# The last up-projection pair of a ConvFFN as a seven-product block pair, joined to a reordered start of the down projection

## The chip, the cores and the metric

One core of one Trainium2 chip runs the whole kernel. The metric is the device time of one execution in microseconds; the figure of a kernel is the median over its runs. Engines are named as in the profile: PE (TensorE, matmuls), DVE (VectorE), ACT (ScalarE), POOL (GpSimd), SP (SyncE, which here only issues DMAs).

## The reference

The reference is one layer of a streaming encoder on 1024 tokens of width 1024: a mixer (attention and a state-space part), and then a gated feed-forward block. All is float32. The change lies in the feed-forward block:

```python
hid = xn @ w_up                                    # 1024 x 5632
hp = jnp.pad(hid, ((0, 0), (CONV_WIDTH - 1, 0), (0, 0)))
conv = conv_b + sum(hp[:, j:j + seq_len] * conv_w[j] for j in range(CONV_WIDTH))
val, gate = jnp.split(conv, 2, axis=-1)
return (jax.nn.silu(gate) * val) @ w_down          # 2816 x 1024
```

The result is added to the residual h, and a last RMSNorm follows.

## The kernel before, in words

Every float32 product is made of three matmuls on split operands: hi·hi, hi·lo and lo·hi. The hi part is a cast (ACT, `S.copy`), the lo part is the difference from it, a subtraction with two operands in SBUF (`split_lo`, L137), on VectorE or GpSimd.

**Up projection.** The 5632 columns of `w_up` are worked as 22 pairs c = 0 to 21; a pair is 128 gate columns and the 128 value columns that belong to them. Pairs 0, 1, 2 and 21 are plain: 144 matmuls 344 or 342 columns wide. Pairs 3 to 20 are block pairs (`block_pair`, `seven`): the 2 × 2 block product of gate and value weights by two halves of the depth and the tokens is made of seven products in place of eight, each on two pieces of 258 and 256 columns, 168 matmuls in all. A block pair needs four sums of weight blocks (GpSimd, `combine`), seven casts and splits, and additions of the results into hg and hv (VectorE, L242). Then the convolution is a scaling on ACT (L1501) and two steps on VectorE for gate and for value, silu on ACT (L1312), a multiplication (L1313; on GpSimd, for the last pair on VectorE), and a store of 128 rows to the DRAM buffer `a_d` (`glue`).

**Down projection.** The 22 row blocks of 128 are joined to eleven j. They are worked in four groups, (8, 9), (7, 0, 1), (2, 3, 4) and (5, 6, 10). A group is again seven products p, in the order 0, 4, 1, 2, 5, 3, 6 (4, 3 and 6 go on in PSUM banks of earlier products), each on four tiles t of 128 tokens, with three matmuls 512 wide for each j. `forms(p, j)` loads the two operands of a product (`ar` of the activations, `wr` of the weights; SP queue), casts them (ACT, L1583) and splits them: on GpSimd for p = 0, 4, 5, else on VectorE. `product` issues the matmuls (L1697 to L1699) and takes the results from PSUM: copies into u2 for the first product, else additions into u2 and hs on VectorE (L1707). The sums of activations for the later groups are on GpSimd too (L1570 to L1576).

A scheduler sorts the instructions of each engine by a simulated timeline. `after(a, b)` puts a behind b in that sorting alone; it is an order, and makes no semaphore between engines. On the chip each engine then works its list from the front.

Of the kernel before, what the change touches and what calls it, by code (L numbers as in the profile page):

```python
# [9 lines left out]
F = mybir.dt.float32  # L10
# [9 lines left out]
P = 128  # L20
# [38 lines left out]
def block_kernel(ctx, tc, x, meta, xbt, x0t, g1t, w_q, w_k, w_v, w_f, w_u, w_g, b_f, w_ao, lam_d, bw_d, cw_d,  # L59
# [142 lines left out]
    def to_feature(xs, n, dhi, dlo, col, bank=st_ps):  # L202
# [9 lines left out]
        return los  # L212

    def m_ps():
        return pp.tile([P, 512], F, tag="mm", name="mm", bufs=3)

    def seven(pl, A, B, kh, pieces, shift, top, bot):
# [26 lines left out]
        for q in st:  # L244
            S.copy(q["c1"], prod(q, "a", m_ps, A11, B11))
        for q in st:
# [1046 lines left out]
    def up_raw(m):  # L1293
        raw = rp.tile([P, KD, P], F, tag="raw", name="raw", bufs=3)
        SY.dma_start(raw, w_up[m])
        return raw
# [14 lines left out]
    def glue(g_, v_, c):  # L1311
        S.activation(g_, g_, AF.Silu)  # L1312
        (V if c == NFF - 1 else GP).tensor_tensor(v_, v_, g_, ALU.mult)  # L1313
        l_, r_ = HALF
        rows = a_d[P * c:P * c + P]
        if c % 2 == 0 and c // 2 in SUMMED:
            SY.dma_start(rows[:, l_], v_[:, l_])
            even[0] = v_
            return
        (S if c == NFF - 1 else SY).dma_start(rows, v_)  # L1320
        if c // 2 not in SUMMED:
            return
        e_, j = even[0], c // 2
        GP.tensor_tensor(e_[:, l_], e_[:, l_], e_[:, r_], ALU.subtract)
        GP.tensor_tensor(g_[:, l_], v_[:, r_], e_[:, l_], ALU.add)
        GP.tensor_tensor(e_[:, r_], v_[:, r_], e_[:, r_], ALU.subtract)
        GP.tensor_tensor(g_[:, r_], g_[:, l_], v_[:, l_], ALU.subtract)
        for p, t_ in ((1, e_[:, l_]), (2, g_[:, l_]), (3, e_[:, r_]), (6, g_[:, r_])):
            SY.dma_start(s_d[p][P * j:P * j + P], t_)

    even, SUMMED = [None], (7, 8, 9)

    def conv_out(m, tag):
        if m % NFF == NFF - 1:
# [106 lines left out]
    HS = LQ - NH  # L1441
    PIECES = [(0, 258), (258, 256)]
    st_t = ExitStack()
    tq = pool(st_t, "tforms", side="left")
    T = [[tq.tile([P, KH, NH], R, name=f"t{i}{w}") for w in "hl"] for i in range(4)]

# [43 lines left out]
    def block_pair(c):  # L1490
# [6 lines left out]
        seven(ha, A, [B11, T3, T2, T1, B21, T4, B22], KH, PIECES, HS, hg, hv)  # L1497
        res = []
        for h_, m, tag in ((hg, NFF + c, "og"), (hv, c, "ov")):
            o = conv_out(m, tag)  # L1500
            S.activation(o, h_[:, :SEQ], AF.Identity, bias=cwc(3, m), scale=cwc(0, m))  # L1501
            for j in (1, 2):
                V.scalar_tensor_tensor(out=o, in0=h_[:, j:SEQ + j], scalar=cwc(j, m), in1=o,  # L1503
                                       op0=ALU.mult, op1=ALU.add)
            res.append(o)
        glue(*res, c)

# [4 lines left out]
    for c in range(3, NFF - 1):  # L1512
        block_pair(c)
    st_t.close()
    plain_pair(NFF - 1)

    down1 = pool(ctx, "down1", side="left")
    small = [down1.tile([P, 4, 512], R, name=f"op{q}") for q in range(4)]  # L1520
    ops = [[t_[:, w] for w in range(4)] for t_ in small]
    ops += featq
    dpool = {}
    pairs = {}
# [5 lines left out]
    def raw_tile(j, k, h_):  # L1530
        if (k, h_) not in pairs.setdefault(j, {}):
            pairs[j][k, h_] = dpool[turn_of[j] % 4 // 2].tile([P, 512], F, tag=f"a{k}{h_}", name="ar", bufs=2)
        return pairs[j][k, h_]

    def behind(ld, j):
        if h_load and j in groups[1]:
            after(ld, h_load[-1])

    LAST = NFF // 2 - 1
    FROM = {0: (0, 0), 4: (1, 0), 5: (1, 1)}  # L1540

# [19 lines left out]
    def forms(p, j):  # L1561
        b_ = down1.tile([P, 512], F, tag="w", name="wr", bufs=8)
        behind(SY.dma_start(b_, w_block(*own_w[p], j) if p in own_w else t_d[p][P * j:P * j + P]), j)
# [30 lines left out]

    first_add, first_copy, cuts = [], [], []

# [81 lines left out]
    def product(g, p, slots, first, last):  # L1678
# [61 lines left out]
    def prepare():  # L1740

        while len(ready) < (len(items) if first_add else 3):
# [7 lines left out]
            ready[g, p] = [forms(p, j) for j in groups[g]]  # L1750

    dpool[0] = down1
# [6 lines left out]
    dn.tile([P, 512], F, tag="a00", name="hold", bufs=2)  # L1759
    sq = dn.tile([P, 512], BF, name="sq")  # L1760
    eps = dn.tile([P, 1], F, name="eps")
    V.memset(eps, EPS)
    u2 = [dn.tile([P, 512], F, name=f"u2{c}") for c in range(4)]
    hs = [dn.tile([P, D], F, name=f"hs{c}") for c in range(4)]
    hs += [dn.tile([P, D], F, name=f"hs{c}") for c in range(4, KD)]
    small2 = [dn.tile([P, 4, 512], R, name=f"op{q}") for q in range(4, 6)]
    ops += [[t_[:, w] for w in range(4)] for t_ in small2]
    for c in range(4):
        h_load.append(SY.dma_start(hs[c], h_d[P * c:P * c + P]))
    for g, p in turns:  # L1770
        prepare()
# [416 lines left out]
```

## Time and profile before

| | us |
|---|---|
| median of 3 runs (1425.15 to 1426.94) | 1426.13 |
| profiled execution, its own time | 1427.24 |
| its span, first to last instruction | 1425.5 |
| PE busy | 1410.6 (99%) |
| DVE busy | 1070.3 (75%) |
| POOL busy | 764.2 (54%) |
| ACT busy | 709.0 (50%) |

Busy times are sums over the whole span, and the mean granted clock of TensorE is 0.998 of full speed. An engine that is busy for less than the span costs time only where another waits for it; so the table says who is full, and the rows further down say where the others come near it.

### The profile page before, as it was taken

To read this page: it belongs to the slowest core of one execution; us is meant where nothing else is said; L and a number is where in the kernel's file an instruction comes from. 1 tells how busy PE (TensorE), PEld (TensorE's weight loads), DVE (VectorE), ACT (ScalarE), POOL (GpSimd) and SP (SyncE) were. 2 spreads that over 40 slices of the span, in tenths; PEclk is the share of its full clock that TensorE was granted. 3 is DMA by queue.
4 is the path that set the end of the run, shared out by engine and by line. 5 is a ranking of instruction groups with operands and counts; after the bars stand their busy time and mean duration, and the time that the engine had idled before them with its cause. 6 is when DMAs were issued, how large, how long until landed. Compare 5 with 4: busy or idle time off the path is not lost.

```text
span 1425.5 us, 26319 instructions
## 1 busy us (share of the span) xinstructions
PE 1410.6 (99%) x9607; PEld 1336.1 (94%) x9607; DVE 1070.3 (75%) x2048; ACT 709.0 (50%) x1381; POOL 764.2 (54%) x872
## 2 busy tenths in 40 slices
PE   8999999999999999999999999999999999999997
PEld 8999999988999999999889999999999999888886
DVE  7999889843667675655479977788886776788867
ACT  7647575423555555534546444344444345644444
POOL 1542257642466556326771334545555545888795
PEclk9999999999999999999999999999999999999999
DMA  8685644530156531087953246666753327864443
GB/s 298 176 203 147 160 106 133 172 119 31 53 156 161 127 111 57 23 287 267 216 161 124 73 114 183 183 173 177 178 142 113 98 79 258 327 205 133 129 94 118
DMA packets 93318, 216.17 MB, mean 152 GB/s; under 512 B 14802, under 2 KB 22610, under 8 KB 92804
## 3 DMA queue, kind: packets, MB, share of 16 engines
q1 hardware_dynamic: 74340, 170.28, 36.3%
q0 software_dynamic: 17696, 41.29, 15.1%
q10 hardware_dynamic: 1152, 2.91, 0.7%
q8 instruction: 76, 1.25, 0.4%
q14 instruction: 54, 0.44, 0.1%
HBM read 170.88 MB, written 71.71 MB: 170 GB/s over the span
## 4 chain that ended last, share of the span: by engine, by line
PE 95%; DMA 2%; issue 1%; ACT 1%; DVE 0%; POOL 0%; POOLq 0%; DVEq 0%; SPq 0%
PE mm L174 5%; PE mm L176 5%; PE mm L175 5%; PE sp L236 4%; PE sp L237 4%; PE sp L238 4%; PE tp L236 3%; PE tp L237 3%; PE tp L238 3%; PE mm L238 3%; PE mm L236 3%; PE mm L237 3%; PE po L966 3%; PE tp L920 2%; PE mm L1699 2%; PE mm L1698 2%
## 5 line engine op out<-in xcount | busy, mean ns | idle before, releaser
L174 PE MATMUL mm<-xhi,whi 128*128 128x342 f32 (+2 forms) x480 | 156.1, 325 | 0.0
L175 PE MATMUL mm<-xlo,whi 128*128 128x342 f32 (+2 forms) x480 | 155.4, 324 | 0.0
L176 PE MATMUL mm<-xhi,wlo 128*128 128x342 f32 (+2 forms) x480 | 154.6, 322 | 0.5 <-DMA wlo<-in_w_g_dram 0.5
L1313 POOL TENSOR_TENSOR ov<-ov,og 128x1024 f32<-128x1024 f32 x21 | 50.8, 2421 | 119.7 <-ACT og L1312 117.4
L137 DVE TENSOR_TENSOR sw<-sf,sw 128x512 fp32r<-128x512 f32 x72 | 73.4, 1020 | 46.2 <-ACT sw L1304 45.1
L1304 ACT CAST sw<-sf 128x512 fp32r<-128x512 f32 x72 | 44.9, 624 | 108.9 <-POOL sf L1451 80.1
L176 PEld LDWEIGHTS mm<-xhi,wlo 128*128 128x128 f32 x480 | 90.4, 188 | 1.3 <-DMA wlo<-in_w_g_dram 0.8
L174 PEld LDWEIGHTS mm<-xhi,whi 128*128 128x128 f32 x480 | 90.4, 188 | 1.1 <-issue 0.6
L175 PEld LDWEIGHTS mm<-xlo,whi 128*128 128x128 f32 x480 | 90.4, 188 | 0.4
L1451 POOL TENSOR_TENSOR sf<-raw,sf 128x512 f32<-128x512 f32 x36 | 62.9, 1748 | 38.8 <-DVE sw L137 38.7
L1451 POOL TENSOR_TENSOR sf<-raw 128x512 f32<-128x512 f32 x36 | 49.1, 1363 | 60.0 <-ACT ov L1361 21.5
L238 PE MATMUL mm<-xhi,sw 128*128 128x258 f32 (+1 forms) x288 | 81.0, 281 | 0.0
L236 PE MATMUL mm<-xhi,sw 128*128 128x258 f32 (+1 forms) x288 | 80.8, 280 | 0.0
L237 PE MATMUL mm<-xlo,sw 128*128 128x258 f32 (+1 forms) x288 | 80.7, 280 | 0.0
L883 ACT ACTIVATE pt<-pt,mx 128x400 f32<-128x400 f32 (+5 forms) x72 | 53.1, 737 | 45.2 <-DVE mx L876 44.9
L1503 DVE SCALAR_TENSOR_TENSOR ov<-hv,cwt,ov 128x1024 f32<-128x1024 f32 x36 | 69.9, 1942 | 0.4 <-ACT ov L1501 0.4
L885 POOL TENSOR_SCALAR pt<-pt,mx 128x400 f32<-128x400 f32 (+5 forms) x72 | 51.8, 721 | 33.3 <-DVE mx L884 28.3
L1304 ACT CAST sw<-raw 128x512 fp32r<-128x512 f32 x70 | 43.0, 621 | 45.0 <-PE sp L238 23.1
L137 DVE TENSOR_TENSOR sw<-raw,sw 128x512 fp32r<-128x512 f32 x70 | 57.9, 831 | 4.3 <-ACT sw L1304 4.0
L137 DVE TENSOR_TENSOR tl<-tp,th 128x512 fp32r<-128x512 f32 (+1 forms) x80 | 50.7, 634 | 12.2 <-ACT th L923 11.6
L923 ACT CAST th<-tp 128x512 fp32r<-128x512 f32 (+1 forms) x80 | 43.4, 543 | 32.1 <-PE tp L920 22.7
L852 POOL CAST qz<-q 64x128 fp32r<-64x128 f32 (+1 forms) x72 | 20.2, 283 | 67.2 <-PE sp L871 65.7
(722 smaller groups left out, 5727.2 us busy)
## 6 DMA issues: line engine op xcount, KB each, us to landing
raw<-in_w_up_dram SPq DMA_DIRECT2D x44, 512.0 KB, 3.7
t_d<-in_w_dn_dram POOLq DMA_DIRECT2D x44, 256.0 KB, 6.9
wr<-t_d SPq DMA_DIRECT2D x44, 256.0 KB, 3.4
ar<-a_d SPq DMA_DIRECT2D x41, 256.0 KB, 5.3
a_d<-ov SPq DMA_DIRECT2D x18, 512.0 KB, 2.6
wr<-in_w_dn_dram SPq DMA_DIRECT2D x33, 256.0 KB, 3.8
t_d<-in_w_dn_dram SPq DMA_DIRECT2D x22, 256.0 KB, 4.3
t_d<-t_d SPq DMA_DIRECT2D x22, 256.0 KB, 4.7
```

The costliest lines, as they stand in the source:

```text
L137: return eng.tensor_tensor(out_, src, hi.bitcast(F), ALU.subtract)
L174: yield PE.matmul(ps, whi[:, i, :], ahi[:, i], start=(i == 0), stop=False)
L175: yield PE.matmul(ps, whi[:, i, :], alo[:, i], start=False, stop=False)
L176: yield PE.matmul(ps, wlo[:, i, :], ahi[:, i], start=False, stop=(i == k - 1))
L236: PE.matmul(ps, a[0][:, i], bh, start=(i == 0 and not joins), stop=False, skip_group_check=True)
L237: PE.matmul(ps, a[0][:, i], bl, start=False, stop=False, skip_group_check=True)
L238: PE.matmul(ps, a[1][:, i], bh, start=False, stop=(i == kh - 1), skip_group_check=True)
L883: ends[:] = rd, S.activation(pt[:n, :kc], pt[:n, :kc], AF.Exp, bias=low, scale=-1.0, accum_out=nm[:n, 0:1])
L885: sc_.append(GP.tensor_scalar(pt[:n, :kc], pt[:n, :kc], nm[:n, 1:2], 1.0, ALU.mult, ALU.mult))
L1304: S.copy(hi, src)
L1451: sums.append(GP.tensor_tensor(f_, a, b, op))
L1503: V.scalar_tensor_tensor(out=o, in0=h_[:, j:SEQ + j], scalar=cwc(j, m), in1=o, op0=ALU.mult, op1=ALU.add)
```

## The change

Pair 21 becomes a block pair. The function of a block pair is cut in two: `block_pair` now ends with hg and hv, and `conv_pair` does the convolution and calls `glue`. For pair 21 the first product of the down projection stands between them in the code. The operands of that product for (8, 9) go into a quarter of the xhi and xlo buffers that is free during the pair, so they are loaded and split earlier. In the order asked for, the two scalings of pair 21 stand ahead of the first copies of product 0, silu behind them; GpSimd's splits for group 1 stand behind all of the splits of group 0 by either engine. The store of pair 21's rows goes from ACT's queue to GpSimd's. The two last additions of product 2 stand behind the splits of product 3.

```diff
@@ seven
-            S.copy(q["c1"], prod(q, "a", m_ps, A11, B11))
+            kept["c1"] = S.copy(q["c1"], prod(q, "a", m_ps, A11, B11))
@@ glue
-        S.activation(g_, g_, AF.Silu)
+        silu = S.activation(g_, g_, AF.Silu)
+        for cp_ in first_copy:
+            after(silu, cp_)
         (V if c == NFF - 1 else GP).tensor_tensor(v_, v_, g_, ALU.mult)
...
-        (S if c == NFF - 1 else SY).dma_start(rows, v_)
+        kept[c] = (GP if c == NFF - 1 else SY).dma_start(rows, v_)
@@ block_pair, cut in two
-        res = []
-        for h_, m, tag in ((hg, NFF + c, "og"), (hv, c, "ov")):
-            o = conv_out(m, tag)
-            S.activation(o, h_[:, :SEQ], AF.Identity, bias=cwc(3, m), scale=cwc(0, m))
+        return hg, hv
+
+    def conv_pair(c, hg, hv, behind=()):
+        res = {}
+        halves = ((hg, NFF + c, "og"), (hv, c, "ov"))
+        for h_, m, tag in halves[::-1] if behind else halves:
+            res[tag] = o = conv_out(m, tag)
+            act = S.activation(o, h_[:, :SEQ], AF.Identity, bias=cwc(3, m), scale=cwc(0, m))
+            if behind:
+                for cp_ in first_copy:
+                    after(cp_, act)
+                for hi in casts[:4]:
+                    after(act, hi)
             for j in (1, 2):
...
     for c in range(3, NFF - 1):
-        block_pair(c)
-    st_t.close()
-    plain_pair(NFF - 1)
...
+        conv_pair(c, *block_pair(c))
...
+    ops = quarter(0, 1)
@@ forms
+            if j in groups[0] and p == 0:
+                after(hi, kept["c1"])
+            elif j in groups[0]:
+                casts.append(hi)
...
+            elif j in groups[1] and p == 0:
+                for hi_ in casts[12:20]:
+                    after(hi, hi_)
...
+            if j in groups[0] and p == 5:
+                fifth.append(cut)
+            elif j in groups[0] and p == 3:
+                third.append(cut)
+            elif j in groups[0] and p == 6:
+                sixth.append(cut)
+            elif j in groups[1] and p == 0:
+                for cut_ in fifth + third + sixth:
+                    after(cut, cut_)
@@ product
+                if first and p == 2 and t > 1:
+                    for cut in third:
+                        after(first_add[-1], cut)
@@ the start of the down projection
-    for p in ORDER[:2]:
+    last_pair = block_pair(NFF - 1)
+    ready[0, 0] = [forms(0, j) for j in groups[0]]
+    st_t.close()
...
+    ops += small + quarter(0, 0) + quarter(1, 0)
+    for p in (4, 1, 2):
         ready[0, p] = [forms(p, j) for j in groups[0]]
...
+    product(0, 0, ready[0, 0], True, False)
+    conv_pair(NFF - 1, *last_pair, behind=cuts)
...
-    for g, p in turns:
+    for g, p in turns[1:]:
         prepare()
```

What this does to the order of the instructions is seen in three places. The first is GpSimd's list from the last splits ahead of the first down product on; `op` and `xlo` are lo parts, `ov` the rows of a pair. Before:

```order
L137 TENSOR_TENSOR op3_14714<-wr_14739,op3_14714 128x512
L137 TENSOR_TENSOR op3_14714<-ar_14741,op3_14714 128x512
L1313 TENSOR_TENSOR ov_14511<-ov_14511,og_14507 128x1024
L137 TENSOR_TENSOR xlo_98<-ar_14870,xlo_98 128x512
L137 TENSOR_TENSOR xlo_98<-wr_14868,xlo_98 128x512
L137 TENSOR_TENSOR xlo_98<-ar_14878,xlo_98 128x512
L137 TENSOR_TENSOR xlo_98<-wr_14876,xlo_98 128x512
L137 TENSOR_TENSOR op1_14712<-ar_14916,op1_14712 128x512
L137 TENSOR_TENSOR xhi_97<-ar_14920,xhi_97 128x512
L1570 TENSOR_TENSOR ar_14916<-ar_14916,ar_14918 128x512
L1574 TENSOR_TENSOR ar_14918<-ar_14922,ar_14918 128x512
```

After:

```order
L137 TENSOR_TENSOR op0_14772<-wr_14784,op0_14772 128x512
L137 TENSOR_TENSOR op0_14772<-ar_14786,op0_14772 128x512
L137 TENSOR_TENSOR op1_14773<-wr_14792,op1_14773 128x512
L137 TENSOR_TENSOR op1_14773<-ar_14794,op1_14773 128x512
L1324 DMA a_d_81<-ov_14868 128x1024
L137 TENSOR_TENSOR op2_14893<-ar_14929,op2_14893 128x512
L137 TENSOR_TENSOR op2_14893<-wr_14927,op2_14893 128x512
L137 TENSOR_TENSOR op3_14894<-ar_14937,op3_14894 128x512
L137 TENSOR_TENSOR op3_14894<-wr_14935,op3_14894 128x512
L137 TENSOR_TENSOR xlo_98<-wr_14991,xhi_97 128x512
L137 TENSOR_TENSOR xlo_98<-wr_14999,xhi_97 128x512
L137 TENSOR_TENSOR xlo_98<-ar_14975,xhi_97 128x512
```

Before, the last pair's rows are not in this list, and from the splits of product 5 (`xlo<-ar_14870` to `xlo<-wr_14876`) GpSimd goes on to splits and sums for group 1. After, the store of pair 21's rows (`DMA a_d_81<-ov_14868`) stands ahead of the splits of product 5 (`op2_14893`, `op3_14894`), and the splits of group 1 (from `xlo_98<-wr_14991` on) directly behind those.

The second place is VectorE's list at the same point, from the multiplication of the last pair (`ov<-ov,og`) on; additions to hs and u take a product from PSUM. Before:

```order
L1313 TENSOR_TENSOR ov_14620<-ov_14620,og_14527 128x1024
L1762 MEMSET eps_14756 128x1
L1707 TENSOR_TENSOR hs0_14762<-hs0_14762,mm_14792 128x512
L1707 TENSOR_TENSOR hs1_14763<-hs1_14763,mm_14793 128x512
L137 TENSOR_TENSOR xlo_98<-ar_14886,xlo_98 128x512
L137 TENSOR_TENSOR xlo_98<-wr_14884,xlo_98 128x512
L137 TENSOR_TENSOR xlo_98<-ar_14894,xlo_98 128x512
L137 TENSOR_TENSOR xlo_98<-wr_14892,xlo_98 128x512
L1707 TENSOR_TENSOR u20_14758<-u20_14758,mm_15004 128x512
L1707 TENSOR_TENSOR hs3_14765<-hs3_14765,po_14795 128x512
L137 TENSOR_TENSOR op4_14770<-ar_14902,op4_14770 128x512
```

After:

```order
L1317 TENSOR_TENSOR ov_14868<-ov_14868,og_14872 128x1024
L1776 TENSOR_TENSOR hs2_14778<-hs2_14778,mm_14838 128x512
L1776 TENSOR_TENSOR hs3_14779<-hs3_14779,po_14839 128x512
L1776 TENSOR_TENSOR u20_14780<-u20_14780,mm_15063 128x512
L1776 TENSOR_TENSOR u21_14781<-u21_14781,mm_15064 128x512
L137 TENSOR_TENSOR xlo_98<-ar_14945,xhi_97 128x512
L137 TENSOR_TENSOR xlo_98<-wr_14943,xhi_97 128x512
L137 TENSOR_TENSOR xlo_98<-ar_14953,xhi_97 128x512
L137 TENSOR_TENSOR xlo_98<-wr_14951,xhi_97 128x512
L1776 TENSOR_TENSOR u22_14782<-u22_14782,mm_15065 128x512
L1776 TENSOR_TENSOR u23_14783<-u23_14783,po_15066 128x512
L137 TENSOR_TENSOR op4_14895<-ar_14961,op4_14895 128x512
```

Before, the four splits of product 3 (`xlo_98<-ar_14886` to `xlo_98<-wr_14892`) follow two additions to hs. After, they stand behind four additions to hs (one of them ahead of the multiplication) and the first two of product 2 to u (`u20`, `u21`).

The third place is TensorE after, where product 3 begins; `mm_15145` and `mm_15146` are the banks of its first two tiles, `po_15066` the last bank of product 2.

```order
L1763 MATMUL po_15066<-xhi_97,xlo_98 128x512
L1761 MATMUL mm_15145<-xhi_97 128x512
L1761 MATMUL mm_15146<-xhi_97 128x512
L1762 MATMUL mm_15145<-xlo_98,xhi_97 128x512
L1763 MATMUL mm_15145<-xhi_97,xlo_98 128x512
L1762 MATMUL mm_15146<-xlo_98,xhi_97 128x512
L1763 MATMUL mm_15146<-xhi_97,xlo_98 128x512
L1761 MATMUL mm_15145<-xhi_97 128x512
L1761 MATMUL mm_15146<-xhi_97 128x512
L1762 MATMUL mm_15145<-xlo_98,xhi_97 128x512
L1763 MATMUL mm_15145<-xhi_97,xlo_98 128x512
L1762 MATMUL mm_15146<-xlo_98,xhi_97 128x512
```

The rows of L1762 read the lo parts of the weights, those of L1763 the lo parts of the activations, which those four splits of VectorE write: the first two splits serve j = 8, the first six rows of product 3, the last two j = 9, from the second `mm_15145<-xhi_97` on. The first matmul of the down projection stands 96 rows ahead of the first row with `mm_15145`; the second row `mm_15145<-xlo_98,xhi_97` is the 104th behind it.

## Rows read from the trace of the kernel before

**Rows 1.** The page: busy times, the chain that ended last, DMA issues to landing.
```profile
PE 1410.6 (99%) x9607; PEld 1336.1 (94%) x9607; DVE 1070.3 (75%) x2048; ACT 709.0 (50%) x1381; POOL 764.2 (54%) x872
...
PE 95%; DMA 2%; issue 1%; ACT 1%; DVE 0%; POOL 0%; POOLq 0%; DVEq 0%; SPq 0%
...
wr<-in_w_dn_dram SPq DMA_DIRECT2D x33, 256.0 KB, 3.8
```

**Rows 2.** TensorE's waits by what they waited for, the longest two.
```profile
PE mm L355 <- ACT uh L413: 5.2, 1, 5.2
PE mm L1208 <- DVE olo L137: 0.6, 1, 0.6
```

**Rows 3.** Stretches: length, busy time by engine (instructions), TensorE's clock, DMA share, GB/s.
```profile
1163.95:1183.93 19.98, 19.98 (x170) 19.98 (x169) 11.87 (x19) 7.59 (x13) 6.81 (x5) 1.00 0.29 102
1183.93:1206.63 22.70, 22.70 (x146) 22.70 (x145) 13.91 (x19) 13.60 (x22) 15.69 (x9) 1.00 0.79 282
1206.63:1244.81 38.18, 38.18 (x171) 31.54 (x170) 28.90 (x36) 24.42 (x47) 26.40 (x18) 1.00 0.91 329
1244.81:1282.99 38.18, 38.18 (x169) 31.52 (x168) 34.19 (x40) 17.44 (x33) 34.22 (x23) 1.00 0.63 202
```

**Rows 4.** Timeline of TensorE (start, length): first matmuls of three stages, and the last.
```profile
1183.93 0.32 PE L1357 MATMUL mm<-xhi,sw 128*128 128x344 f32 x1
...
1206.63 0.40 PE L1697 MATMUL mm<-op 128*128 128x512 f32 x1
...
1244.81 0.39 PE L1697 MATMUL sp<-op 128*128 128x512 f32 x1
...
1417.07 0.28 PE L1699 MATMUL mm<-xlo 128*128 128x224 f32 x1
```

**Rows 5.** Timelines of VectorE and ScalarE: last addition, multiplication, scaling.
```profile
1184.29 0.42 DVE L242 TENSOR_TENSOR hg<-tp,hg 128x256 f32<-128x256 f32 x1
...
1211.28 1.23 DVE L1313 TENSOR_TENSOR ov<-ov,og 128x1024 f32<-128x1024 f32 x1
...
1181.81 1.24 ACT L1501 ACTIVATE ov<-hv,cwt 128x1024 f32<-128x1024 f32 x1 [8.21 <-DVE hv L242]
```

**Rows 6.** GpSimd issuing DMAs: one in its timeline, and four (min/median/max ns).
```profile
1081.91 0.83 POOL L1469 DMA_DIRECT2D t_d<-in_w_dn_dram  x1
...
L1709 POOL DMA_DIRECT2D hs<-h_d x4: 907/1301/1627, 1351.5 to 1358.5; - x4
```

**Rows 7.** Timeline of GpSimd, first down group: alone, and beside VectorE.
```profile
1216.32 1.29 POOL L137 TENSOR_TENSOR xlo<-wr,xlo 128x512 fp32r<-128x512 f32 x1
1217.57 1.30 POOL L137 TENSOR_TENSOR xlo<-ar,xlo 128x512 fp32r<-128x512 f32 x1
...
1225.76 1.84 POOL L1570 TENSOR_TENSOR ar<-ar 128x512 f32<-128x512 f32 x1
```

**Rows 8.** Timeline of VectorE, first down group.
```profile
1221.65 0.68 DVE L137 TENSOR_TENSOR xlo<-wr,xlo 128x512 fp32r<-128x512 f32 x1
...
1225.17 0.67 DVE L1707 TENSOR_TENSOR hs<-hs,po 128x512 f32<-128x512 f32 x1
1225.76 0.68 DVE L137 TENSOR_TENSOR op<-ar,op 128x512 fp32r<-128x512 f32 x1
1226.37 1.78 DVE L137 TENSOR_TENSOR op<-wr,op 128x512 fp32r<-128x512 f32 x1
1228.07 1.78 DVE L137 TENSOR_TENSOR op<-ar,op 128x512 fp32r<-128x512 f32 x1
```

**Rows 9.** Timeline of VectorE, second down group: a split and an addition.
```profile
1244.97 1.19 DVE L137 TENSOR_TENSOR xlo<-ar,xlo 128x512 fp32r<-128x512 f32 x1
...
1246.68 1.19 DVE L137 TENSOR_TENSOR xlo<-wr,xlo 128x512 fp32r<-128x512 f32 x1
```

**Rows 10.** Timeline of VectorE: the ends of a stretch of 28 instructions.
```profile
1230.37 0.67 DVE L1707 TENSOR_TENSOR u<-u,mm 128x512 f32<-128x512 f32 x1
...
1255.29 0.67 DVE L1707 TENSOR_TENSOR u<-u,tp 128x512 f32<-128x512 f32 x1
```

More of the change, by code (lines that the diff above doesn't have):

```diff
@@ L212, in to_feature @@
         return los
+    kept = {}
     def m_ps():
@@ L1442, in block_kernel @@
     PIECES = [(0, 258), (258, 256)]
+    down0 = pool(ctx, "down0", side="left")
+    for tag in ("a00", "w"):
+        down0.tile([P, 512], F, tag=tag, name="hold", bufs=2)
+    eps = down0.tile([P, 1], F, name="eps")
+    V.memset(eps, EPS)
     st_t = ExitStack()
     tq = pool(st_t, "tforms", side="left")
-    T = [[tq.tile([P, KH, NH], R, name=f"t{i}{w}") for w in "hl"] for i in range(4)]
+    T = {i: [tq.tile([P, KH, NH], R, name=f"t{i}{w}") for w in "hl"] for i in (1, 2, 0, 3)}
+    T = [T[i] for i in range(4)]
     sums = []
@@ L1512, in block_kernel, with quarter, weight_tile, raw_buffer @@
     for c in range(3, NFF - 1):
-        block_pair(c)
-    st_t.close()
-    plain_pair(NFF - 1)
[L1519 to L1523, printed above, removed]
+        conv_pair(c, *block_pair(c))
+    def quarter(r, h_):
+        cols = slice((L - 512) * h_, (L - 512) * h_ + 512)
+        return [[t_[:, KH * r + 2 * q + w, cols] for w in range(2) for t_ in (xhi, xlo)] for q in range(2)]
+    ops = quarter(0, 1)
+    n_w = [0]
+    def weight_tile():
+        n_w[0] += 1
+        if n_w[0] % 8 in (1, 2):
+            return down0.tile([P, 512], F, tag="w", name="wr", bufs=2)
+        return down1.tile([P, 512], F, tag="w", name="wr", bufs=6)
+    def raw_buffer(j, tag):
+        pl = dpool[turn_of[j] % 4 // 2]
+        if pl is dpool[0] and tag == "a00":
+            pl = down0
+        return pl.tile([P, 512], F, tag=tag, name="ar", bufs=2)
+    def op_tiles(pl, q0, q1):
+        small = [pl.tile([P, 4, 512], R, name=f"op{q}") for q in range(q0, q1)]
+        return [[t_[:, w] for w in range(4)] for t_ in small]
+    dpool = {0: None}
     pairs = {}
@@ L1531, in raw_tile @@
         if (k, h_) not in pairs.setdefault(j, {}):
-            pairs[j][k, h_] = dpool[turn_of[j] % 4 // 2].tile([P, 512], F, tag=f"a{k}{h_}", name="ar", bufs=2)
+            pairs[j][k, h_] = raw_buffer(j, f"a{k}{h_}")
         return pairs[j][k, h_]
+    first_loads = []
     def behind(ld, j):
-        if h_load and j in groups[1]:
+        if h_load and len(first_loads) == 16:
             after(ld, h_load[-1])
+        if j in groups[1]:
+            after(ld, first_loads[-1])
+        if j in groups[0]:
+            after(ld, first_loads[-1] if first_loads else kept["raw"])
+            first_loads.append(ld)
     LAST = NFF // 2 - 1
@@ L1561, in forms @@
     def forms(p, j):
-        b_ = down1.tile([P, 512], F, tag="w", name="wr", bufs=8)
+        b_ = weight_tile()
         behind(SY.dma_start(b_, w_block(*own_w[p], j) if p in own_w else t_d[p][P * j:P * j + P]), j)
@@ L1593, in forms @@
         return slot
-    first_add, first_copy, cuts = [], [], []
+    first_add, cuts, late_casts, fifth, third, sixth, casts = [], [], [], [], [], [], []
     held = {}
@@ L1758, in block_kernel @@
     gfB = dn.tile([P, D], F, name="gfB")
-    dn.tile([P, 512], F, tag="a00", name="hold", bufs=2)
+    for tag in ("a00", "a01", "a10", "a11"):
+        dn.tile([P, 512], F, tag=tag, name="hold", bufs=2)
+    hs.update((c, dn.tile([P, D], F, name=f"hs{c}")) for c in (7, 6))
     sq = dn.tile([P, 512], BF, name="sq")
[L1761 to L1769, printed above, removed]
-    for g, p in turns:
+    ops += op_tiles(dn, 2, 4) + quarter(1, 1) + op_tiles(dn, 4, 6)
+    hs.update((c, dn.tile([P, D], F, name=f"hs{c}")) for c in (4, 5))
+    cuts.clear()
+    ops += ready[0, 0]
+    for g, p in turns[1:]:
         prepare()
```

47 lines of the change are left out of this document (36 added, 11 removed).

## The prediction

> **What bounds the kernel now.** I read the page first. TensorE is busy for 1410.6 us of a span of 1425.5, and the chain that ended last is 95% TensorE [rows 1]. The list of TensorE's waits confirms it: after one wait of 5.2 us at the start, the largest is 0.6 us [rows 2]. So the time is the sum of the matmuls' own times, plus the start and a tail; another engine matters only where it makes TensorE wait.
>
> The table by stretches shows the stage that changes. Each of its four stretches is full of TensorE at a granted clock of 1.00, while VectorE and GpSimd work for parts of it: 11.87 and 6.81 us in block pair 20, 13.91 and 15.69 in the plain pair, 28.90 and 26.40 in the first down group, 34.19 and 34.22 of 38.18 in the second [rows 3]. That pair of engines becomes tight exactly where the change moves work. The edges are TensorE's own: block pair 20 runs from 1163.95 to 1183.93, the plain pair 21 to 1206.63, and the first down group's 168 matmuls to 1244.81 [rows 3, 4].
>
> **The matmuls.** Pair 21 has 144 matmuls in 22.70 us (157.6 ns each). As a block pair it has 168 narrower ones; pair 20, the same shape, takes 19.98 us (118.9 ns each). The difference is 22.70 − 19.98 = **2.72 us saved**, less than 0.2% of the time. The down products keep their number and width, 38.18 / 168 = 0.2273 us each. Nothing else in the diff removes work from TensorE, so 2.72 us is the most that can be won.
>
> The first down matmul then stands at 1183.93 + 19.98 = 1203.91 us on the clock of before. I call this T0; a matmul n places on is due at T0 + 0.2273 n.
>
> **What is hidden.** The new pair's four weight sums on GpSimd and seven cast and split pairs are those of pair 20, during which TensorE lost nothing [rows 3]. The last addition of a block pair comes 0.36 us after its last matmul and takes 0.42 (1184.29 against 1183.93) [rows 4, 5], so hv and hg are complete at about T0 + 0.8 = 1204.7. One scaling of 1.24 us [rows 5] stands after that and ahead of the first copies: 1205.9, and the first copy follows by 1206.5. Its bank is wanted again by the matmul 24 places on (T0 + 5.46 = 1209.4), so 2.9 us of slack remain; without that cover the scaling would cost its 1.24 us. Silu and the multiplication on VectorE (1.23) [rows 5] run in the first product's shadow; the multiplication stands behind an addition to hs that waits for the matmul 51 places on (T0 + 11.6 + 0.4 = 1215.9), so it ends at about 1217.8. Up to here I find no wait of TensorE.
>
> **GpSimd after the store.** The store of pair 21's rows is now on GpSimd's queue and waits for that multiplication. Behind it stand the four splits of product 5 and then group 1's splits. Issuing a DMA holds GpSimd for 0.83 us in one place and a median of 1.30 in another [rows 6]. With 0.83 the four splits, 1.29 each in a pitch of 1.25 [rows 7], run from 1218.7 to **1223.7**, and group 1's follow at once. Nothing in the order makes them wait for VectorE's splits of group 0: "follow" is a place in the schedule, without a semaphore between the two engines.
>
> **VectorE at the same moment.** Its four splits of product 3 stand behind the additions of product 2, tiles 0 and 1. The second of those needs the matmul 83 places on, due at 1222.8 and 0.4 long [rows 4], and with 0.6 of its own ends at **1223.8**. The split of the second pair's weights is needed by the product-3 matmul 104 places on, due at T0 + 23.66 = **1227.57**. Alone, such a split takes 0.68 us (1221.65), and the next can start 0.60 after it, as at 1225.76 and 1226.37 [rows 8]: four of them end by 1226.2, and TensorE doesn't wait.
>
> But they are not alone. Where both engines run additions with two operands in SBUF, before shows them taking turns. GpSimd and VectorE both start at 1225.76; VectorE takes 0.68 and GpSimd 1.84. VectorE's next, from 1226.37, takes 1.78 and ends at 1228.15, after GpSimd's has ended at 1227.60, and the one from 1228.07 takes 1.78 again [rows 7, 8]. One turn of each is 1.70 us. An addition with an operand in PSUM takes 0.67 beside the same GpSimd work (1225.17) and isn't held up. So the four splits end at 1223.8 + 0.68 + 3 × 1.70 = 1229.6 if VectorE goes first, or about 1.1 later, 1230.7, if GpSimd does. Against 1227.57 that is a stall of 2.0 to 3.1 us. Both engines are ready within 0.1 us; the nearest row, 1225.76, lets VectorE go first, so I take **2.2 us**. Bounds: nothing (GpSimd idle) and 3.1.
>
> The Trainium skill, SBUF — State Buffer, "Who interferes with whom", says that a VectorE instruction with two SBUF inputs contends with a GpSimd instruction that reads SBUF, and that whichever issues first keeps the shared port for its whole length. The rows from 1226.37 on agree, with 1.78 us against 0.68. By that rule GpSimd, ready at 1223.7, would go first, and the sum would end 0.9 us higher than mine.
>
> **The next group.** The next tight place is group 1's first product: the addition of its tile 2 must empty a PSUM bank for the matmul 222 places on (1254.4 plus the stall, 1256.6). From 1229.8 on, VectorE has 14 splits and 13 additions ahead of and with it. At 1.71 us for one split and one addition together (1244.97 to 1246.68, with GpSimd working) [rows 9] they end at about 1253.7; if no addition hides in GpSimd's turn, 13 × 0.6 later, 1261.5. In before a like mixture (12 splits, 16 additions, the first and the last at 1230.37 and 1255.29) took 25.6 us [rows 10]; two splits more and three additions fewer make 25.6 + 2 × 1.19 − 3 × 0.6 = 26.2, and so 1256.0. I count **0**, bounds 0 and 4.9.
>
> **Sum.** 1427.24 − 2.72 + 2.2 = 1426.7 for the profiled execution, which lies 1.11 above the median of the runs shown (1426.13). On the median: 1426.13 − 2.72 + 2.2 = **1425.6 us**. The tail of 8.4 us from the start of the last matmul, at 1417.07 [rows 4], is untouched.
>
> **Rivals.**
> - *No stall.* GpSimd is not there when VectorE splits: a load of group 1 or its cast lands late, since those loads stand on SP behind the earlier ones. For it: a weights load takes a median of 3.8 us from issue to landing [rows 1], and ScalarE's queue is long. Against it: the splits of product 5, which don't depend on them, already reach 1223.7. It gives 1426.13 − 2.72 = 1423.4.
> - *Half a stall.* Two turns of GpSimd fall between VectorE's four splits, not three: 1223.8 + 0.68 + 2 × 1.70 + 0.6 = 1228.5, a stall of 0.9; 1424.3.
> - *Slower.* The taking of turns goes on through group 1: each addition that no longer hides costs 0.6 us at the bank of tile 2. With six of the 13, 3.6 us are added: 1425.6 + 3.6 = 1429.2. It decides the sign from the point where more than 0.5 us of that reaches TensorE, and passes 0.2% from 3.4 us. For it: both engines are busy for 34.2 of 38.18 us there [rows 3]. Against it: before carried the same splits in the same stretch with no wait listed [rows 2].
> - *The change does nothing for TensorE's sum.* Excluded, unless the block pair's matmuls are slower here than in pair 20.
>
> **Chances.** My forecast (own range 1424.9 to 1426.5) 0.45; no stall 0.25; half a stall 0.15; slower 0.15. What a measurement of this kernel can tell from no change is about 0.2%, 2.85 us: faster means below 1423.3, slower above 1429.0. Faster comes only from a little under half of the no-stall case, 0.11; slower from some two thirds of the last, 0.10; the same, 0.79. The range goes from 1423.1, leaving out a third of the no-stall case, to 1428.1, leaving out most of the slower one: together about 0.2.
>
> **What would show it.** The last up pair's 168 matmuls within 20.0 us, the first down matmul 2.7 us earlier. Then TensorE waiting, once or twice, for VectorE's lo splits in product 3, in all 1.5 to 3 us; VectorE's splits there at 1.7 to 1.8 us each, with GpSimd's lo splits between; GpSimd idle before its store, until about 1217.8. No such wait, with VectorE's splits at 0.68, is the first rival; a wait for an addition to u in group 1 of over 2 us is the slower one. A wait for the first copies or the scalings would break the step that I count as hidden.

## The result

The changed kernel takes 1427.97 us (median of 20 runs, 1425.78 to 1431.85), the kernel before 1426.01 (20 runs, 1425.04 to 1428.12): a ratio of 1.0015, 95% interval 1.0008 to 1.0022. That is slower by 2 us, clear of the noise, though inside the 0.2% that I called the same. I had forecast 1425.6.

The profiled execution after took 1427.61 us, its span 1425.8. The page's busy times, and then the list of TensorE's waits (us in total, times, longest):

```profile
PE 1411.4 (99%) x9631; PEld 1333.8 (94%) x9631; DVE 1079.9 (76%) x2053; ACT 712.2 (50%) x1384; POOL 775.0 (54%) x877
```

```profile
PE mm L357 <- ACT uh L415: 4.8, 1, 4.8
PE mm L1762 <- DVE xlo L137: 1.0, 1, 1.0
PE mm L1210 <- DVE olo L137: 0.4, 1, 0.4
```

The second line is new: TensorE waits for a lo split of VectorE in product 3, as I had named it, once. TensorE's timeline gives the edges, to be held against [rows 4]:

```profile
1183.64 0.28 PE L238 MATMUL mm<-xhi,sw 128*128 128x258 f32 x1
...
1203.61 0.40 PE L1761 MATMUL mm<-xhi 128*128 128x512 f32 x1
...
1417.87 0.27 PE L1763 MATMUL mm<-op 128*128 128x224 f32 x1
```

The last up pair takes 1203.61 − 1183.64 = 19.97 us, 2.73 less than in [rows 3]. But the down projection, from its first to its last matmul, takes 1417.87 − 1203.61 = 214.26, against 1417.07 − 1206.63 = 210.44 before: 3.82 more, of which a single wait of 1.0 us explains about a quarter. The stretches (columns as in [rows 3]) are the last up pair, the down projection up to the first matmul of the second group, and a piece of about the same length behind that:

```profile
1183.64:1203.61 19.97, 19.97 (x171) 19.97 (x169) 9.81 (x15) 9.09 (x16) 13.71 (x9) 1.00 0.46 156
1203.61:1242.15 38.54, 37.58 (x164) 30.32 (x163) 31.77 (x37) 27.69 (x49) 22.20 (x16) 1.00 0.98 360
1242.15:1281.00 38.85, 38.85 (x170) 31.69 (x169) 37.33 (x42) 20.44 (x38) 34.65 (x23) 1.00 0.72 234
```

The third is the clue: TensorE is never idle in it, at a granted clock of 1.00, and yet its matmuls start 230.2 ns apart, where those of the last stretch in [rows 3] start 227.6 apart. The matmuls themselves stand further apart. Here are six in a row on xhi, first in before, then after; same width, no wait among them in either:

```profile
1253.70 0.39 PE L1697 MATMUL sp<-xhi 128*128 128x512 f32 x1
1253.93 0.39 PE L1698 MATMUL sp<-xhi 128*128 128x512 f32 x1
1254.16 0.39 PE L1699 MATMUL sp<-xhi 128*128 128x512 f32 x1
1254.38 0.39 PE L1697 MATMUL sp<-xhi 128*128 128x512 f32 x1
1254.61 0.39 PE L1698 MATMUL sp<-xhi 128*128 128x512 f32 x1
1254.84 0.39 PE L1699 MATMUL sp<-xhi 128*128 128x512 f32 x1
1255.06 0.39 PE L1697 MATMUL tp<-op 128*128 128x512 f32 x1
```

```profile
1260.10 0.40 PE L1761 MATMUL mm<-xhi 128*128 128x512 f32 x1
1260.34 0.40 PE L1762 MATMUL mm<-xlo,xhi 128*128 128x512 f32 x1
1260.57 0.39 PE L1763 MATMUL mm<-xhi,xlo 128*128 128x512 f32 x1
1260.80 0.39 PE L1761 MATMUL mm<-xhi 128*128 128x512 f32 x1
1261.03 0.39 PE L1762 MATMUL mm<-xlo,xhi 128*128 128x512 f32 x1
1261.26 0.39 PE L1763 MATMUL mm<-xhi,xlo 128*128 128x512 f32 x1
1261.49 0.40 PE L1761 MATMUL mm<-op 128*128 128x512 f32 x1
```

From first to last 1.36 us before (0.2267 each), 1.39 after (0.2317). Over the whole down projection I took the distance from the start of each 512-wide matmul to the start of the next, without those above 245 ns, which I call gaps: 227.59 ns before, 230.42 after. Times 904 such distances that is 2.56 us; the two gaps (1225.99 to 1227.69) add 1.24 us beyond 227 ns each. Together 3.80 of the 3.82.

So the two traces differ by −2.73 (pair), +2.56 (distance) and +1.24 (wait), or +1.1; with 0.2 elsewhere, nearly all of it in the 18 block pairs that both kernels have, it is 1.28 us from the kernel's first matmul to its last. The profile after is one of the quicker of its runs and the one of before one of the slower of its own; what the other 0.7 us of the medians is, one trace doesn't show, and 1.28 us lies within the interval of the ratio (1.1 to 3.1 us). The runs of after spread over 6 us, those of before over 3. Part of such a spread arises ahead of the block pairs: from the first matmul of the kernel to theirs it takes 819.0 us in this trace of before, and 817.1 to 818.3 in those of three runs below (e4, f1, f4) whose matmuls and operands are the same up to there.

### The profile page after: what moved, and what is told of

Its sections match the earlier page's. It is cut to its first block, busy times and chain, and to the rows that moved or that the text cites. A ratio compares the mean times of both kernels' runs of the same rounds, so it can differ in the third digit from the quotient of the medians.

```text
span 1425.8 us, 26382 instructions
## 1 busy us (share of the span) xinstructions
PE 1411.4 (99%) x9631; PEld 1333.8 (94%) x9631; DVE 1079.9 (76%) x2053; ACT 712.2 (50%) x1384; POOL 775.0 (54%) x877
## 4 chain that ended last, share of the span: by engine, by line
PE 96%; DMA 2%; DVE 1%; ACT 1%; issue 0%; SPq 0%; POOL 0%; POOLq 0%; DVEq 0%; ACTq 0%
PE mm L174 6%; PE mm L175 5%; PE mm L176 5%; PE sp L238 5%; PE sp L239 5%; PE sp L240 5%; PE tp L238 3%; PE tp L239 3%; PE tp L240 3%; PE mm L239 3%; PE mm L238 3%; PE mm L240 3%; PE po L968 3%; PE tp L922 2%; PE mm L1762 2%; PE mm L1763 2%
## 5 line engine op out<-in xcount | busy, mean ns | idle before, releaser
L137 DVE TENSOR_TENSOR sw<-sf,sw 128x512 fp32r<-128x512 f32 x76 | 76.6, 1008 | 47.1 <-ACT sw L1306 46.9
L1459 POOL TENSOR_TENSOR sf<-raw,sf 128x512 f32<-128x512 f32 x38 | 67.3, 1772 | 38.7 <-DVE sw L137 38.3
L1459 POOL TENSOR_TENSOR sf<-raw 128x512 f32<-128x512 f32 x38 | 52.2, 1374 | 62.2 <-ACT ov L1363 21.5
L240 PE MATMUL mm<-xhi,sw 128*128 128x256 f32 (+1 forms) x304 | 85.5, 281 | 0.0
L238 PE MATMUL mm<-xhi,sw 128*128 128x256 f32 (+1 forms) x304 | 85.3, 281 | 0.0
L239 PE MATMUL mm<-xlo,sw 128*128 128x256 f32 (+1 forms) x304 | 85.3, 280 | 0.0
```

Of the source, the lines that this page charges most:

```text
L137: return eng.tensor_tensor(out_, src, hi.bitcast(F), ALU.subtract)
L238: PE.matmul(ps, a[0][:, i], bh, start=(i == 0 and not joins), stop=False, skip_group_check=True)
L239: PE.matmul(ps, a[0][:, i], bl, start=False, stop=False, skip_group_check=True)
L240: PE.matmul(ps, a[1][:, i], bh, start=False, stop=(i == kh - 1), skip_group_check=True)
L1459: sums.append(GP.tensor_tensor(f_, a, b, op))
```

## The experiments

Two questions: why are the matmuls further apart, and what does the wait for the lo splits cost? The table holds all runs (the ratio is against the kernel before, run beside it; the rest is from each profile: length of the down projection, mean distance and gaps as above). Each set of experiments had its own runs of the kernel before, with medians of 1426.24 to 1426.66, so the ratios can be compared, the medians only roughly. The addresses named below are those that the build assigns.

| run | median us | ratio (95%) | down us | ns apart | gaps us |
|---|---|---|---|---|---|
| before | 1426.01 | | 210.44 | 227.59 | 0 |
| after | 1427.97 | 1.0015 (1.0008 to 1.0022) | 214.26 | 230.42 | 1.24 |
| e1_op_aligned | 1430.10 | 1.0024 (1.0015 to 1.0033) | 215.71 | 230.97 | 2.23 |
| e2_rows_paired | 1428.63 | 1.0016 (1.0007 to 1.0025) | 215.03 | 231.35 | 1.18 |
| e3_both_aligned | 1430.19 | 1.0026 (1.0016 to 1.0035) | 217.84 | 231.11 | 4.22 |
| e4_before_aligned | 1425.70 | 0.9992 (0.9984 to 1.0001) | 210.43 | 227.59 | 0 |
| f1_before_one_phase | 1425.66 | 0.9995 (0.9986 to 1.0004) | 209.63 | 226.70 | 0 |
| f2_before_all_64 | 1426.73 | 1.0002 (0.9993 to 1.0011) | 209.63 | 226.70 | 0 |
| f4_before_op_128 | 1426.46 | 1.0001 (0.9992 to 1.0010) | 210.40 | 227.52 | 0 |
| f3_after_one_phase | 1430.18 | 1.0020 (1.0010 to 1.0029) | 218.57 | 227.19 | 8.49 |
| g1_after_ten_slots | 1426.78 | 1.0006 (0.9997 to 1.0015) | 214.15 | 229.53 | 1.97 |
| g2_ten_slots_wait | 1427.95 | 1.0009 (1.0000 to 1.0018) | 215.12 | 229.45 | 3.01 |
| g3_after_wait | 1428.77 | 1.0018 (1.0006 to 1.0029) | 215.93 | 230.51 | 2.85 |
| g4_after_store_sp | 1428.18 | 1.0013 (1.0004 to 1.0022) | 216.59 | 230.51 | 3.52 |
| h1_after_migrated | 1425.05 | 0.9992 (0.9983 to 1.0001) | 212.72 | 227.61 | 2.27 |
| h2_migrated_wait | 1425.84 | 0.9996 (0.9987 to 1.0005) | 211.14 | 227.60 | 0.69 |

**First guesses: alignment.** The change moves operands. Its `eps` tile, 32 bytes ahead of the op tiles, shifts all six of them by 32, where before only the last two stood so; and `quarter` takes an operand slot's weights and moving operand from neighbouring rows of xhi and xlo, 4160 bytes apart, where before a slot was one piece of 8 KB.

```diff
e1  - eps = down0.tile([P, 1], F, name="eps")
    + eps = down0.tile([P, 16], F, name="eps")[:, :1]
e2  - return [[t_[:, KH * r + 2 * q + w, cols] for w in range(2) for t_ in (xhi, xlo)] for q in range(2)]
    + return [[t_[:, KH * r + q + 2 * w, cols] for w in range(2) for t_ in (xhi, xlo)] for q in range(2)]
e3  both of them
e4  (in before)
    - eps = dn.tile([P, 1], F, name="eps")
    + eps = dn.tile([P, 16], F, name="eps")[:, :1]
```

> The changed kernel with the one-column tile ahead of the op tiles made 64 bytes wide in place of 32, so that all op tiles start at a multiple of 64 bytes; nothing else differs, no instruction and no order. Theory A (the down matmuls take 230.4 ns in place of 227.6 because the op tiles now start 32 bytes off): the matmuls whose operands lie in op fall to about 227, the mean pitch by 1.3 to 2.6 ns, and the time by 1.2 to 2.5 us, to 1425.5 to 1426.8. Theory B (it is the hi and lo parts in the quarters of xhi and xlo, whose weights and moving operands start 64 bytes apart modulo 128): the matmuls on xhi and xlo keep 230 and the time falls by less than 0.8. Theory C (it is the denser work of the other engines and DMAs in these stretches): no change, 1428.0.

> The changed kernel with the rows of a quarter taken as 0 and 2, 1 and 3 for a slot's weights and moving operand, in place of 0 and 1, 2 and 3: both then start at the same address modulo 128 bytes. No instruction and no order differs. Theory B: the matmuls on xhi and xlo fall from 230.2 to about 227 ns, and the time by 1.3 to 2 us, to about 1426.2; both places mended together would give 2.5. Theory A and theory C: no change, 1428.0. If hi and lo parts in two tiles far apart are what costs, no change either.

> Both placements together in the changed kernel. Theories A and B together: all down matmuls at 226.7 to 227.6 ns, the time 2.5 to 3.2 us lower than the changed kernel's, 1424.8 to 1425.5, that is 0.5 to 1.2 below the kernel before; what is left to the 2.72 of the block pair is the wait of TensorE for the lo splits, 1.2 to 1.4 us. Theory C: 1428.0.

> The kernel before with its one-column tile 64 bytes wide, so that the op tiles 4 and 5, which start 32 bytes off a multiple of 64, come onto one; nothing else differs. Theory A or A with B: its matmuls on op 4 and 5 and those just behind fall from 229 to 235 ns to 226.7, in all 0.8 us, 1425.2. Theory C: no change, 1426.0.

Theories A and B both fell: 64-byte starts (e1), starts equal modulo 128 (e2) and both together leave the distance at 231 ns, and in e4 the last two op tiles stayed slow at their new place. e1's ratio can't be told from after's, since the intervals overlap; its profile is 2.3 us longer, 1.0 of it in longer gaps, 0.5 in the distance, and 0.3 in the block pairs, where operands moved by 32 bytes too (e3, which moves them likewise, has the same 0.3). The rest lies ahead of the block pairs. But before has a pattern that theory C does not explain: its distance is 226.7 ns through whole products, leaves that value exactly when TensorE comes to op 4 or 5, and finds it again some matmuls after leaving them. All its other full-width operands start at the same address modulo 512 bytes (192); op 4 and 5 at 224, in e4 at 256.

**One phase.** Hence theory D: what counts is whether all operands start at one address modulo 512.

```diff
f1  (in before; eps goes behind op 4 and 5)
    - eps = dn.tile([P, 1], F, name="eps")
    - V.memset(eps, EPS)
      u2 = [dn.tile([P, 512], F, name=f"u2{c}") for c in range(4)]
...
      ops += [[t_[:, w] for w in range(4)] for t_ in small2]
    + eps = dn.tile([P, 1], F, name="eps")
    + V.memset(eps, EPS)
f2  f1, and ahead of xhi
    + xp.tile([P, 16], F, name="gap")
f4  f1, and ahead of the op tiles
    + down1.tile([P, 32], F, name="gap")
f3  (in after; eps as in f1, slots as in before from product 2 on)
    + def rows_of(t_, c0):
    +     return [[flat(t_)[:, c0 + 2048 * q + 512 * w:c0 + 2048 * q + 512 * w + 512] for w in range(4)] for q in range(2)]
...
    - ops += small + quarter(0, 0) + quarter(1, 0)
    + ops += small + quarter(0, 0) + rows_of(xhi, 4224)
...
    - ops += op_tiles(dn, 2, 4) + quarter(1, 1) + op_tiles(dn, 4, 6)
    + ops += op_tiles(dn, 2, 4) + rows_of(xlo, 4224) + op_tiles(dn, 4, 6)
...
    - ops += ready[0, 0]
...
    - ops += ready[g, p]
    + ops += rows_of(xhi, 0) + rows_of(xlo, 0) if (g, p) == (0, 1) else ready[g, p]
```

> The kernel before with its one-column tile moved behind the op tiles 4 and 5, so that every operand of the down projection starts at the same address modulo 512 bytes (192); in before, and in the run with that tile widened, op 4 and 5 alone differ, and there alone the pitch leaves 226.7 ns. Theory D (the pitch is 226.7 ns where all operands have that one phase modulo 512, and about 230 where they differ or it is another): all down matmuls at 226.7, the down projection 0.8 us shorter, 209.6, and the time about 1425.3. Theory C (denser work of the other engines): 227.6, no change.

> The same, with xhi, xlo and all behind them 64 bytes further on: one phase, but another one (256). If only equal phases count, 226.7 ns as in the run beside it. If the phase itself counts (192 or 64 modulo 128 is good), about 229 to 230 ns in all of the down projection, 2 to 3 us more than the run beside it, and other stages may change with it. Theory C: no change.

> The changed kernel with the layout of before for the operands of the down projection: from product 2 on they lie in one piece in xhi or in xlo, and the one-column tile is behind the op tiles, so that all but 48 of its matmuls have phase 192. Theory D: the mean pitch falls from 230.4 to about 227 ns, the down projection is 2.5 to 3 us shorter, and the time is about 1425.2, with the waits for lo splits (1.2 us) still there; other waits can move a little, since a group's operands come free at other times. Theory C: 230.4 ns, 1428.

> The kernel with one phase, with all op tiles 128 bytes further on: xhi and xlo at 192, op at 320 modulo 512. If the phase counts modulo 128, 226.7 ns everywhere, as without the shift. If it counts modulo 256 or 512, 228 to 231 ns around and in op, about 1 to 2 us more. Theory C: no change.

f1 is the clean answer: no instruction more or less, one small tile elsewhere, and all but five of its 906 full-width matmuls are 226 or 227 ns from the next; the down projection is 0.81 us shorter, as expected. Its median can't tell so little from nothing (the interval of its ratio includes 1). Its timeline on op 4 and 5, six distances that make 1.36 us, and the same six in before, 1.40:

```profile
1240.00 0.39 PE L1697 MATMUL mm<-op 128*128 128x512 f32 x1
1240.22 0.39 PE L1698 MATMUL mm<-op 128*128 128x512 f32 x1
1240.45 0.39 PE L1699 MATMUL mm<-op 128*128 128x512 f32 x1
1240.68 0.39 PE L1697 MATMUL mm<-op 128*128 128x512 f32 x1
1240.90 0.39 PE L1698 MATMUL mm<-op 128*128 128x512 f32 x1
1241.13 0.39 PE L1699 MATMUL mm<-op 128*128 128x512 f32 x1
1241.36 0.39 PE L1697 MATMUL mm<-op 128*128 128x512 f32 x1
```

```profile
1242.03 0.40 PE L1697 MATMUL mm<-op 128*128 128x512 f32 x1
1242.27 0.40 PE L1698 MATMUL mm<-op 128*128 128x512 f32 x1
1242.50 0.40 PE L1699 MATMUL mm<-op 128*128 128x512 f32 x1
1242.74 0.39 PE L1697 MATMUL mm<-op 128*128 128x512 f32 x1
1242.96 0.39 PE L1698 MATMUL mm<-op 128*128 128x512 f32 x1
1243.19 0.40 PE L1699 MATMUL mm<-op 128*128 128x512 f32 x1
1243.43 0.39 PE L1697 MATMUL mm<-op 128*128 128x512 f32 x1
```

f2 shows that the phase's own value doesn't matter (another one, 226.7 again; its profile is 1.6 us longer than f1's ahead of the down projection, 0.7 of it in the 18 block pairs, where operands moved as well, and most of the rest ahead of them, where traces vary by more). f4 shows that equality modulo 128 isn't enough: most passages between op and xhi or xlo (48 of 58), 128 apart, cost two longer distances, as 232 and 231 ns, 10 ns in all; but for three short places it is 226.7 inside each set. f3 shows the mended distance in the changed kernel, 227.19, but its gaps grew to 8.49 us: the order of the instructions of its group 1 is another one, and TensorE waits for VectorE twice.

```profile
PE sp L1762 <- DVE u L1777: 2.9, 1, 2.9
PE tp L1762 <- DVE hs L1777: 2.9, 1, 2.9
```

So f3 settles the distance, and not the time.

**The wait.** Four runs in the changed kernel's own order.

```diff
g1  f3 without the last three lines of its edit (ops += ready[0, 0] and ops += ready[g, p] stay)
g2  g1, and
g3  after, and (in forms, where the splits of group 1 are ordered)
    + tc.add_manual_dep(cut.ins, third[-1].ins.name, mybir.DependencyInfo(
    +     mybir.DependencyClass.Sync, mybir.DependencyReason.DATA), reason="port")
g4  (in after)
    - kept[c] = (GP if c == NFF - 1 else SY).dma_start(rows, v_)
    + kept[c] = SY.dma_start(rows, v_)
```

> The changed kernel in its own order, with ten of the fourteen operand slots at phase 192 modulo 512 (those in rows 4 to 7 of xhi and xlo laid in one piece, the one-column tile behind the op tiles); the four in rows 0 to 3 keep their mixed phases. Theory D: the mean pitch falls from 230.4 to between 227.5 and 229 ns, the down projection loses 1.3 to 2.6 us, and, as no other wait is new, the time is 1425.6 to 1426.7. If the run with the layout of before was slow for its layout and not for its later waits, this one is slow too, 1428 or more.

> The same, and GpSimd's splits for group 1 wait, by a semaphore, for VectorE's last split of product 3. Taking turns at the port is the cause of TensorE's wait for lo splits: that wait (1.0 us, 1.2 in the matmuls' starts) is gone, GpSimd stands still until about 1226 and loses little, since its third split waited until 1228.1 anyway; 1.2 us below the run without the semaphore, 1424.4 to 1425.5, below the kernel before. If another thing delays the splits, the wait stays; if GpSimd's lateness matters, a new wait in group 1 takes the gain back.

> The changed kernel with that semaphore alone. The wait for lo splits goes, the pitch stays at 230.4 ns: 1426.7, 1.2 us below the changed kernel. If the wait has another cause, 1428.0.

> The changed kernel with the store of pair 21's rows on SP's queue: GpSimd doesn't stand behind VectorE's multiplication, its splits of product 5 run from about 1215 to 1220 and the two ready ones of group 1 end by 1222.5, ahead of VectorE's splits at 1223.8. If GpSimd's lateness is what brings the two together, the wait for lo splits goes, and the time falls by about 1.2 us to 1426.7; SP's loads behind the store are hardly later. If GpSimd is in the way all the same, with the next splits of group 1, the wait stays: 1428.0.

g1 mended a third of the distance (229.53, less than expected, for its mixed slots alternate with the others through group after group), and its ratio fell from 1.0015 to 1.0006 with the wait for lo splits still there. The two intervals overlap, though, and in its profile longer gaps take back the gain: the down projection is as long as after's.

The semaphore does what it should: VectorE's four splits run at a pitch of 0.60 (g3's timeline of VectorE), and the wait for lo splits is gone. But the time doesn't fall, for another wait has come, for additions to u in group 1 (g3's list of waits):

```profile
1223.38 0.68 DVE L137 TENSOR_TENSOR xlo<-ar,xhi 128x512 fp32r<-128x512 f32 x1
1223.98 0.68 DVE L137 TENSOR_TENSOR xlo<-wr,xhi 128x512 fp32r<-128x512 f32 x1
1224.59 0.68 DVE L137 TENSOR_TENSOR xlo<-ar,xhi 128x512 fp32r<-128x512 f32 x1
1225.19 0.68 DVE L137 TENSOR_TENSOR xlo<-wr,xhi 128x512 fp32r<-128x512 f32 x1
```

```profile
PE sp L1763 <- DVE u L1778: 2.0, 2, 1.1
```

g2 has the same (2.2 us in two), and so has g4, in which GpSimd stands behind no store: no wait for lo splits, but 0.8 us for u and 1.4 for hs, and 3.52 us of gaps. In all three the 1.2 us that TensorE no longer waits at 1226 it waits later, and the gaps are in all 1.0 to 2.3 us longer than without the edit. The expectations of a gain were wrong; their clause on a new wait in group 1 came true.

**Both together, as far as they go.** h1 keeps group 0 as in after and lays the four remaining slots in one piece after their use in group 1; all but 96 matmuls are then at one phase.

```diff
h1  g1, and
    + mixed = ready[0, 0] + ready[0, 1]
...
    - ops += ready[g, p]
    + if g < 1 or (g, p) not in ((1, 0), (1, 4)):
    +     ops += ready[g, p]
    + else:
    +     ops += [s_ for s_ in ready[g, p] if not any(s_ is o_ for o_ in mixed)]
    + if (g, p) == (1, 4):
    +     ops += rows_of(xhi, 0) + rows_of(xlo, 0)
h2  h1 with the semaphore of g2
```

> The changed kernel with all but 96 of its 942 down matmuls at phase 192 modulo 512: as in the run with ten slots, and the four slots in rows 0 to 3 are laid in one piece once group 1 has used them. Its order differs from the changed kernel's in group 1 only. Theory D accounts for the changed kernel's loss: the mean pitch is 227 to 227.6 ns, the down projection 2.5 to 3 us shorter than the changed kernel's for it, and with waits of 1.2 to 2 us the time is 1425.0 to 1426.0, at or a little below the kernel before. If the pitch is mended and the time stays at 1427 or more, the gain goes into waits of TensorE for VectorE in group 1, as in the run with the layout of before.

> The same with GpSimd's splits for group 1 behind VectorE's last split of product 3 by a semaphore. In the two earlier runs with it the wait in product 3 went and waits of 2 to 3 us for additions to u came in group 1. If VectorE and GpSimd together are the limit there, the same again: no gain, 0 to 1 us more than the run without it. If a shorter pitch gives them no less time than it takes from TensorE, 1 us less.

h1's distance is that of before, 227.61, and its down projection is 1.54 us shorter than after's in spite of 1.0 us more of gaps. Its ratio, 0.9992 (0.9983 to 1.0001), lies wholly below after's (1.0008 to 1.0022): laying the operands at one phase undoes the loss. Of the 3.0 us by which its profile is shorter, 1.5 lie in the down projection and 0.3 in the block pairs; the rest lies ahead of the block pairs, where traces vary by nearly 2 us. That is the version that the experiments point to, but that it beats the kernel before is not shown: the interval includes 1, and e4, whose distance is that of before, has the same ratio. h2 has the shortest gaps of the changed kernels in its profile (0.69 us, a span of 1421.1), but its runs go from 1422.9 to 1427.6 with a median of 1425.84: the semaphore took 1.6 us of gaps out of this profile and nothing off the median, and what decides is open.

## Why the prediction was wrong

- **The bound**, right: TensorE is full in every run, and the time is the sum of its matmuls and waits.
- **The matmuls**: the pair saved 2.73 us, against 2.72. The step that failed is "The down products keep their number and width, 38.18 / 168 = 0.2273 us each". They kept both and came to stand 0.2304 us apart, since their operands moved to addresses of different phase: +2.56 us, nearly the whole gain of the pair. I had read `quarter` and the `eps` tile as bookkeeping, and costed their effect on TensorE at nothing without a row for it; before carried the row, in the two op tiles at which its own distance rises to 230.
- **What is hidden**, right: no wait for the scalings, the first copies or the multiplication.
- **The wait in product 3**: right in product and engines; in after's profile it is smaller (1.24 us against 2.2), and it stands six matmuls earlier: the 98th from the first waits for the first pair's splits, where I had the 104th wait for the second's (in e1 and e3 both wait). VectorE lost once there, not three times by turns: GpSimd's first two splits of group 1 ran back to back, and the third was not ready.

```profile
1223.61 2.54 POOL L137 TENSOR_TENSOR xlo<-wr,xhi 128x512 fp32r<-128x512 f32 x2
1228.12 5.04 POOL L137 TENSOR_TENSOR xlo<-ar,xhi 128x512 fp32r<-128x512 f32 x3 [1.98 <-ACT xhi L1626]
```

```profile
1223.78 2.91 DVE L137 TENSOR_TENSOR xlo<-ar,xhi 128x512 fp32r<-128x512 f32 x1
1226.62 0.68 DVE L137 TENSOR_TENSOR xlo<-wr,xhi 128x512 fp32r<-128x512 f32 x1
```

The split from 1223.78 ends at 1226.69, 0.54 after GpSimd's pair has ended at 1226.15: it held off for both. Here the start of GpSimd, 0.17 us ahead, decided; I had let a tie in [rows 8] decide otherwise. The Trainium skill (SBUF — State Buffer, "Who interferes with whom") has it that whoever issues first keeps the port for its whole instruction; here that held, and for the instruction behind it too. But 1.24 is one trace's size. In e1, e2 and e3, with the same order of instructions, the gaps in product 3 come to 2.23, 1.18 and 3.26 us, for GpSimd's next splits of group 1 meet VectorE's at other moments. In e1 they start at 1228.44, and VectorE's fourth split is held off as well, 1.78 us in place of 0.68:

```profile
1228.79 1.78 DVE L137 TENSOR_TENSOR xlo<-wr,xhi 128x512 fp32r<-128x512 f32 x1
```

So 2.2 lies within what this order gives; to count on one size was too much. (104 matmuls at 0.2273 make 23.64, not 23.66; that changes nothing.)
- **The next group**: 0 was right for the changed kernel, and the place was right: take the wait in product 3 away (g2, g3, g4), and TensorE waits in group 1 for VectorE, 2.0 to 2.2 us by the lists of waits. My slower rival named it, but as an addition to the first wait, where it is its alternative.
- **The sum**: −2.72 + 2.2 was forecast, −2.73 + 1.24 + 2.56 came in the traces. That the range held the median (its end 1428.1 against 1427.97) is luck: that end stood for further waits, the sign was wrong, and no rival of mine had the mechanism that made it so.

## What to carry to other kernels

Where TensorE is full, count the distance of its matmuls and not only their number: a change that moves operands can cost over 1% of every matmul with no idle time, no wait and a full clock to show for it. What removed that here was to lay all operands of a stretch of matmuls at one address modulo 512 bytes, with the small tiles behind the large ones. And a wait that vanishes when an engine's order is mended has gained nothing until the next place where the same two engines meet is seen to have room.

## What the runs showed of the hardware that I had not expected

- Back-to-back 512-wide matmuls of this kernel start 226.7 ns apart when all operands start at one address modulo 512 bytes, whichever it is (f1 at 192, f2 at 256). A step of 128 between two such sets costs 10 ns at most passages (f4). With a step of 32 (before) or 64 (e4) the distances on the set that stands apart are between 224 and 236 ns for as long as it lasts. Mixed within a product, as in after, they are 230.4 on average. Steps of 256 were not tried, and why it is so no run shows.
- Moves of operands show in the block pairs of the up projection too, by less. The 18 that all kernels share take 359.55 or 359.56 us in f3, g1, g2, h1 and h2, 359.81 in after, e2, g3 and g4, whose `eps` tile shifts some of their operands by 32 bytes, and 360.08 in e1 and e3, which shift them by 64. In the one layout of before, e4, f1 and f4 they vary from 359.56 to 359.65.
- A wait can cost more than itself. Behind f3's second gap, of 3.3 us to 1299.70, the next matmuls start 0.43 us apart, and the granted clock over the stretch is 0.66, with 1.00 in a stretch ahead of the gap. That is about twice their distance, as at the lower of the clock's two levels (1.2 GHz), and it adds 1.6 us. Behind f3's first gap, as long (1249.93 to 1253.24), the granted clock was 1.00 and the distance 0.23 from the second matmul on; what makes the difference no run shows.

```profile
1253.00:1258.00 5.00, 4.76 (x21) 3.96 (x22) 4.55 (x7) 4.43 (x9) 5.00 (x4) 1.00 0.54 179
...
1290.00:1296.00 6.00, 6.00 (x28) 4.95 (x28) 6.00 (x1) 1.80 (x4) 6.00 (x6) 1.00 0.33 90
1299.00:1304.00 5.00, 4.30 (x12) 3.44 (x13) 5.00 (x8) 1.24 (x2) 3.74 (x3) 0.66 0.54 157
...
1300.29 0.63 PE L1763 MATMUL tp<-xlo 128*128 128x512 f32 x1
1300.72 0.63 PE L1764 MATMUL tp<-xlo 128*128 128x512 f32 x1
```
